# Hybrid encoder trunk: two of the four recurrent units of a layer run their chunks in step, and x is fetched in one layout for its first norm

## The chip, the cores and the metric

The kernel runs on one core of one Trainium2 chip. The metric is the device time of one launch in microseconds (us), as the median of several runs. TensorE (PE in the profile) has a clock of two levels, 1.2 and 2.4 GHz; the profile gives the granted level as a share, 0.50 or 1.00.

## The reference, cut to what matters

Two layers work on x, 256 tokens by 2048 channels in f32. Each layer normalises x, multiplies it by a 2048 by 14784 matrix, and feeds four branches of width 512:

```python
h = _rms_norm(x, norm_g[l])       # x * rsqrt(mean(x*x) + 1e-6) * g
p = h @ w_in[l]
y_a = _rwkv7_bidir(...)           # 8 heads of 64, one scan over tokens in each direction
y_b = _diff_attention(...)        # differential attention
y_c = _mla(...)                   # latent attention
y_d = _mem_attention(...)         # attention into 256 memory tokens
z = sum(sigmoid(merge_b) * ((y_b * silu(gate_b)) @ w_branch[l, b]))
x = x + z @ w_out[l]
```

The recurrent branch y_a updates a 64 by 64 state per head and direction with every token; afterwards each head is normalised over its 64 channels.

## The kernel before, in words

Every large product is done as three fp32r products: `split` writes a rounded high part and the remainder of both operands (for weights the tiles `whi` on ScalarE and `wlo` on VectorE, line 95 in the profile, since a metering wrapper calls the engine there). `main` is the lane of these products. It walks a list of jobs in a fixed order: keys and values of the memory branch (`in_mem_w_kv`, two jobs of 16 contraction tiles), then the products with `w_in`, the small ones of the latent attention, branch products, and `w_out`. A job with `("hT", l)` as its condition is only written into the program once the normalised and transposed x exists.

Beside `main` run seven lanes: norms of the memory, parameters and `z_prep`, norms of x (`x_prep`, for layer 0 `x_first`), tables, attention, latent attention, and the recurrent branch (`rwkv`). They are generators; a loop in `build` takes them in turns, with assumed times for PE, VectorE and ScalarE, and so sets the order in which instructions are written; a scheduler of the framework with priorities sets the final order on each engine. On the chip each engine runs its instructions strictly in that order.

`x_first` in layer 0 needs one factor per token, rsqrt(mean(x*x)+eps). It fetches x twice: as `xT` (channels on partitions, four pieces of 512 KB into tiles U and ygh, which held the memory's pieces until then) and as `x` (tokens on partitions, two pieces of 1 MB into Z). `token_sums` squares and sums the latter on ScalarE in four pieces with an accumulator, takes `rsqrt` of 2 columns on GpSimd with the power operation, and `x_first` then spreads the factor, transposes it on PE (line 161) and copies it to the tile `r4` (`rb`; the profile drops the digit and names it r). All 16 tiles of xT are multiplied by gain and factor on VectorE, and split into T1h and T1l, the moving operands of the first `w_in` job.

`rwkv` calls `rw_unit` for four units of two heads one after another. A unit has a preparation (decay, keys, the products PR, a triangular inverse in `rw_inverse`, whose result is TT), then four steps n over chunks of 64 tokens, in which both directions advance: products R, their copy, products SA with TT, their copies, products SP and Y, and the state update on VectorE. All use PSUM tiles `pr`, of which there are two; Y holds one of them during the steps. Then comes the head norm of the unit.

Start of the launch: small memory fills on GpSimd (`ticks`) pace the first transfers; `tick(i, dst)` lets a transfer start after fill i. The first two memory tiles have raised priority.

Of the kernel before, what the change touches and what calls it, by code (L numbers as in the profile page):

```python
# [10 lines left out]
F32 = mybir.dt.float32  # L11
# [5 lines left out]
ALU = mybir.AluOpType  # L17
# [28 lines left out]
XE = 5.0  # L46
# [66 lines left out]
class Builder:  # L113
# [71 lines left out]
    def setup(self):  # L185
        nc, a = self.nc, self.a
        self.cst = self.cp.tile([128, C_N], F32, name="cst")
        self.ident = self.cst[:, C_ID:C_ID + 128]
        self.G = self.cp.tile([128, 2, 4, 65], F32, name="G")
        self.ticks = [nc.gpsimd.memset(self.G, 1.0).ins]  # L190
        self.ones = self.cp.tile([128, 2], F32, name="ones")
        nc.gpsimd.memset(self.ones, 1.0)
        with self.tc.high_priority(2 * HP):
            nc.scalar.activation(self.small(2), self.ones, AF.Exp)
            warm = self.t("PT", [128, 2, 256], bufs=1)[:, 0]
            nc.vector.memset(warm, 0.0)
# [3 lines left out]
        self.TT = self.cp.tile([128, 2, 4, 64], F32, name="TT")  # L200
        self.ticks.append(nc.gpsimd.memset(self.TT, 0.0).ins)
        self.ST = [self.cp.tile([128, 2, 2, 64], F32, name=f"ST{i}") for i in range(2)]
        for s in self.ST:
# [140 lines left out]
    def mem_prep(self, l):  # L344
# [22 lines left out]
        for i in range(8):  # L367
            if not l and 1 <= i <= 4:
                with self.tc.issue_after(self.last[0]):
                    load(i + 3)  # L370
            if not l and i == 3:
                with self.tc.issue_after(self.fetch):
                    nc.sync.dma_start(self.cst, a["consts"])
            for kk in (2 * i, 2 * i + 1):
                j, k = kk // 4, kk % 4
                with self.tc.high_priority(2 * HP if kk < 4 else 0):
# [24 lines left out]
    def x_first(self):  # L401
# [140 lines left out]
    def main(self):  # L542
# [7 lines left out]
        def prepare(upto):  # L550
            while nxt[0] < len(flat) and nxt[0] <= upto:
# [161 lines left out]
    def e_merge(self, l, b, j):  # L713

        def f(tt, ps):
# [59 lines left out]
    def z_prep(self, l):  # L775

        parts = self.v["zT", l] = []
        for i, tags in enumerate((("q1",), ("k1",), ("V1",), ("iA",), ("X",), ("BK", "qr"), ("T1h",), ("T1l",))):
# [304 lines left out]
    def rwkv(self, l):  # L1083
# [3 lines left out]
        for ft in range(4):  # L1087
            yield from self.rw_unit(l, ft, U)
# [8 lines left out]
    def rw_unit(self, l, ft, U):  # L1097
# [26 lines left out]
        X = self.t("X", [128, 2, 4, 128])  # L1124
        nc.gpsimd.memset(X[64:128, :, 0:4:2], 0.0)
        nc.gpsimd.memset(X[0:64, :, 1:4:2], 0.0)
        pv = self.pr().rearrange("p (a f) -> p a f", a=4)
        for c in range(2):
            self.mm(pv[:, c], v[:, c * 128:c * 128 + 128], cst[:, C_CEN:C_CEN + 128])
        for d in range(2):  # L1130
            self.copy(X[0:64, d, 0:4:2], pv[0:64, 0:2])
            nc.vector.tensor_copy(X[64:128, d, 1:4:2], pv[64:128, 0:2])
# [11 lines left out]
        G = self.G  # L1144
        AR = self.t("S2", [128, 2, 4, 2, 64])
        BKT = self.t("S3", [128, 2, 4, 128])
        PR = [self.t(f"S{d}", [128, 4, 2, 128]) for d in range(2)]
        kds = self.t("kds", [128, 256])
# [10 lines left out]
        for d in range(2):  # L1159
# [55 lines left out]
        yield from self.rw_inverse(PR)  # L1215


        TT = self.TT
        Y = self.pr()[:, :256]
        st = None  # L1220
        for n in range(4):
# [5 lines left out]
            def kp(c):  # L1227
                return slice(64, 128) if c % 2 else slice(0, 64)

            R = self.pr()[:, :128].rearrange("p (h i) -> p h i", h=2)  # L1230
            if n:
                for d, c in dc:
                    self.mm(R[bp(c)].rearrange("p h i -> p (h i)"), AR[:, d, c, 0],
                            st[:, d].rearrange("p h i -> p (h i)"), True, False)
            for hb in range(2):
                hs = slice(hb * 64, hb * 64 + 64)
                for d, c in dc:
                    self.mm(R[bp(c), hb], PR[d][:, ci(c), hb, 0:64], X[:, d, c, hs], not n, n == 0 or hb == 1)
            Rs = self.t("Rs", [128, 2, 64], bufs=2)
            self.copy(Rs, R)  # L1240
            yield
            SA = self.pr()[:, :128].rearrange("p (h i) -> p h i", h=2)
            for hb in range(2):
                for d, c in dc:
                    self.mm(SA[bp(c), hb], TT[bp(c), d, (c // 2) * 2 + hb], Rs[bp(c), hb])
            for d, c in dc:
                o = X[bp(c), d, c].rearrange("p (h i) -> p h i", h=2)
                if d == 0:
                    self.copy(o, SA[bp(c)])
                else:  # L1250
                    nc.vector.tensor_copy(o, SA[bp(c)])
            yield
            if n < 3:
                SP = self.pr()[:, :128].rearrange("p (d i) -> p d i", d=2)
                for d, c in dc:
                    for hb in range(2):
                        hs = slice(hb * 64, hb * 64 + 64)
                        self.mm(SP[hs, d], BKT[:, d, c, hs], X[:, d, c, hs])
            for d, c in dc:
                first, final = (n == 0 and d == 0), (n == 3 and d == 1)  # L1260
                cs = slice(c * 64, c * 64 + 64)
                for hb in range(2):
                    hs = slice(hb * 64, hb * 64 + 64)
                    self.mm(Y[hs, cs], X[:, d, c, hs], PR[d][:, ci(c), hb, 64:128], first, final and not n)
                for hb in range(2):
                    hs = slice(hb * 64, hb * 64 + 64)
                    if n:
                        self.mm(Y[hs, cs], st[:, d, hb], AR[:, d, c, 1], False, final)
            if n < 3:
                o0, o1 = n * 65 + 64, 260 + (3 - n) * 65  # L1270
                gc = G.rearrange("p d c t -> p (d c t)")[:, o0:o1 + 1:o1 - o0]
                new = self.ST[n % 2]
                gb = gc[:, :, None].to_broadcast([128, 2, 64])
                for hb in range(2):
                    hs = slice(hb * 64, hb * 64 + 64)
                    src = SP[hs]
                    if n:
                        nc.vector.tensor_tensor(new[hs, :, hb], src, st[hs, :, hb], op=ALU.add)
                        src = new[hs, :, hb]
                    nc.vector.tensor_tensor(new[hs, :, hb], src, gb[hs], op=ALU.mult)  # L1280
                st = new
            yield


        sq = self.t("sq", [128, 256])
        nc.scalar.activation(sq, Y, AF.Square)
        yg = self.t("r2", [128, 256], bufs=2)
        self.copy(yg, Y, scale=col(P_GG + ft))
        yield
# [11 lines left out]
        bv = self.t("r3", [128, 256], bufs=2)  # L1301
# [5 lines left out]
        nc.vector.tensor_tensor(yg, yg, ps, op=ALU.mult)  # L1307
# [3 lines left out]
    def rw_inverse(self, PR):  # L1311
# [4 lines left out]
        TT = self.TT  # L1316
# [231 lines left out]
```

## Time and profile before

| what | value |
|---|---|
| median of 3 runs | 2039.52 us (2034.0 to 2042.97) |
| profiled execution, its time | 2035.4 us |
| its span (first to last instruction) | 2033.5 us |
| PE busy | 2016.3 us, 99% of the span, 12066 matmuls |
| VectorE, ScalarE, GpSimd busy | 70%, 55%, 8% |
| DMA | 369.45 MB, mean 182 GB/s |

A busy PE in this profile need not be at its peak: the ends of matmuls are modelled, and consecutive ones overlap in the record. What a matmul occupies is read from start to start of its neighbours.

### The profile page before, as it was taken

The page shows a single profiled execution, that of the slowest core. Times are in us where ns is not written, and L with a number is a line of the kernel's source. Part 1 is how long each engine was busy: PE and PEld are TensorE (multiplying, and loading weights), DVE is VectorE, ACT ScalarE, POOL GpSimd, SP SyncE. Part 2 cuts the span into 40 slices and gives each one's busy share as a digit, 9 for nine tenths or more (in the row PEclk, how much of TensorE's full clock was granted, in tenths as well). Part 3 has the DMA queues.
Part 4 walks back from the last instruction along what each step waited for, and adds up shares of the span by engine and source line. Part 5 has one row for each costly group of instructions (what it writes and reads, how often), then busy time and mean ns, then how long its engine had stood idle before and what let it go on. Part 6 is the DMA issues. An engine that isn't in the chain of part 4 may idle for free.

```text
span 2033.5 us, 33805 instructions
## 1 busy us (share of the span) xinstructions
PE 2016.3 (99%) x12066; PEld 1695.8 (83%) x12066; DVE 1417.8 (70%) x3070; ACT 1118.1 (55%) x2317; POOL 152.9 (8%) x174
## 2 busy tenths in 40 slices
PE   8999999999999999999999999999999999999999
PEld 6998997887877888777889988888778778877887
DVE  5878888986587577558565658666656876765664
ACT  5756565655455445446465556765555554444543
POOL 1201100210010000000000010110011001000000
PEclk9999999999999999999999999999999999999999
DMA  8665655566455556656765656455555555665565
GB/s 298 215 183 157 189 173 171 148 186 186 141 181 165 169 171 191 198 171 226 237 191 179 182 156 179 147 164 175 161 181 166 176 157 158 197 200 165 183 201 190
DMA packets 222585, 369.45 MB, mean 182 GB/s; under 512 B 40592, under 2 KB 60816, under 8 KB 221840
## 3 DMA queue, kind: packets, MB, share of 16 engines
q1 hardware_dynamic: 218736, 356.31, 57.8%
q10 hardware_dynamic: 3456, 10.49, 1.3%
q8 instruction: 95, 1.56, 0.3%
q0 software_dynamic: 224, 0.49, 0.2%
q14 instruction: 74, 0.61, 0.1%
HBM read 359.88 MB, written 11.53 MB: 183 GB/s over the span
## 4 chain that ended last, share of the span: by engine, by line
PE 91%; issue 3%; DVE 2%; DMA 2%; ACT 1%; SPq 0%; POOL 0%; ACTq 0%; DVEq 0%; POOLq 0%
PE mm L156 81%; PE pr L156 5%; PE pa L156 3%; PE pa L161 2%; DMA raww<-in_mem_w_kv 1%; DVE wlo L95 1%; PE pr L161 0%; DVE S L95 0%; DMA raww<-in_w_in 0%; DMA U<-in_memT 0%; ACT whi L95 0%; SPq L1375 0%; DVE Z L95 0%; DVE BK L95 0%; POOL small L179 0%
## 5 line engine op out<-in xcount | busy, mean ns | idle before, releaser
L95 ACT ACTIVATE whi<-raww 128x512 fp32r<-128x512 f32 (+2 forms) x1300 | 786.7, 616 | 738.3 <-PE mm L156 407.0
L95 DVE TENSOR_TENSOR wlo<-raww,whi 128x512 fp32r<-128x512 f32 (+2 forms) x1300 | 863.9, 675 | 449.7 <-ACT whi L95 439.2
L156 PE MATMUL mm<-wlo,T1h 128*128 128x512 f32 (+2 forms) x1440 | 564.6, 392 | 2.6 <-DVE wlo L95 2.6
L156 PE MATMUL mm<-whi,T1l 128*128 128x512 f32 (+2 forms) x1472 | 566.1, 388 | 0.0
L156 PE MATMUL mm<-whi,T1h 128*128 128x512 f32 (+2 forms) x1472 | 537.7, 391 | 1.3 <-ACT whi L95 1.2
L156 PEld LDWEIGHTS mm<-whi,T1h 128*128 128x128 f32 x1472 | 275.3, 188 | 57.1 <-ACT whi L95 2.1
L156 PEld LDWEIGHTS mm<-whi,T1l 128*128 128x128 f32 x1472 | 276.5, 188 | 51.8 <-issue 0.3
L156 PEld LDWEIGHTS mm<-wlo,T1h 128*128 128x128 f32 x1440 | 270.6, 188 | 57.8 <-DVE wlo L95 5.1
L156 PE MATMUL mm<-T1l,whi 128*128 128x256 f32 x960 | 272.4, 285 | 0.4 <-DVE T1l L95 0.4
L156 PE MATMUL mm<-T1h,wlo 128*128 128x256 f32 x960 | 272.6, 286 | 0.0
L156 PE MATMUL mm<-T1h,whi 128*128 128x256 f32 x960 | 272.5, 285 | 0.0
L156 PEld LDWEIGHTS mm<-T1l,whi 128*128 128x128 f32 x960 | 183.6, 191 | 1.6 <-DVE T1l L95 0.6
L156 PEld LDWEIGHTS mm<-T1h,whi 128*128 128x128 f32 x960 | 183.6, 192 | 1.2
L156 PEld LDWEIGHTS mm<-T1h,wlo 128*128 128x128 f32 x960 | 183.0, 191 | 0.8
L156 PE MATMUL mm<-wlo,ygh 128*128 128x512 f32 (+1 forms) x296 | 116.5, 396 | 0.0
L156 PE MATMUL mm<-whi,ygl 128*128 128x512 f32 (+1 forms) x296 | 115.6, 393 | 0.0
L156 PE MATMUL mm<-whi,ygh 128*128 128x512 f32 (+1 forms) x296 | 110.0, 395 | 0.0
L156 PE MATMUL mm<-whi,S 128*128 128x512 f32 x256 | 86.5, 414 | 5.0 <-ACT whi L95 4.8
L179 POOL TENSOR_TENSOR small<-small,cst 128x4 f32<-128x4 f32 (+3 forms) x46 | 52.3, 1139 | 514.1 <-DVE small L95 430.1
L156 PEld LDWEIGHTS mm<-whi,ygl 128*128 128x128 f32 x296 | 55.6, 188 | 12.3 <-issue 1.0
L156 PEld LDWEIGHTS mm<-whi,S 128*128 128x128 f32 x256 | 50.0, 198 | 19.1 <-ACT whi L95 7.6
L156 PEld LDWEIGHTS mm<-whi,ygh 128*128 128x128 f32 x296 | 55.6, 188 | 12.3 <-issue 1.0
(279 smaller groups left out, 2165.8 us busy)
## 6 DMA issues: line engine op xcount, KB each, us to landing
raww<-in_w_in SPq DMA_DIRECT2D x432, 512.0 KB, 3.6
raww<-in_w_branch SPq DMA_DIRECT2D x64, 512.0 KB, 4.5
raww<-in_w_out SPq DMA_DIRECT2D x64, 512.0 KB, 4.6
raww<-in_mem_w_kv SPq DMA_DIRECT2D x29, 512.0 KB, 3.6
raww<-in_w_in SPq DMA_DIRECT2D x16, 384.0 KB, 3.6
raww<-in_w_in SPq DMA_DIRECT2D x16, 320.0 KB, 3.7
raww<-in_w_in SPq DMA_DIRECT2D x16, 256.0 KB, 2.8
Z<-in_x ACTq DMA_DIRECT2D x2, 1024.0 KB, 6.9
```

The lines of the kernel that those rows point to most:

```text
L95: return g(out, *args, **kw)
L156: return self.nc.tensor.matmul(out, lhsT=lhsT, rhs=rhs, start=start, stop=stop).ins
L161: self.nc.tensor.transpose(out, in_, self.ident[:k, :k])
L179: self.nc.gpsimd.tensor_tensor(ss, ss, self.cst[:, C_MH:C_MH + n], op=ALU.pow)
```

## The change

- `x_first` fetches only xT. It squares the four pieces on ScalarE (128 by 1024 each), adds them on VectorE down to 128 by 256, sums over partitions with one product with a matrix of ones, scales, and applies the power of -0.5 on GpSimd to the whole 128 by 256 tile, against a tile filled with -0.5.
- The third and fourth unit of each layer are prepared one after the other; then `rw_chunks` takes both through their steps: in each step the products R of both units, then SA of both, then SP and Y of both, with PSUM tiles that hold both. The second of the pair has its own G, TT and ST, and uses S4, S5, S6 of the latent attention (and kds2, BKT, iA), so it waits for `("gatefree", l, 1)`, the end of the latent attention's heads.
- BKT, the transposed keys, is made for three chunks of a direction, not four, since the last is not used.
- The group norm's gain moves from the copy of Y into the later multiplication. The recurrent branch's merge gates go to q1, k1, V1, and `z_prep` takes its tiles in another order.
- At the start, ticks of the paced transfers are one fill earlier, and only two, no longer four, of the first memory tiles have raised priority. The scratch of GpSimd's transfers is halved.

```diff
-        self.G = self.cp.tile([128, 2, 4, 65], F32, name="G")
-        self.ticks = [nc.gpsimd.memset(self.G, 1.0).ins]
+        self.G = [self.cp.tile([128, 2, 4, 65], F32, name=f"G{i}") for i in range(2)]
+        self.ticks = [nc.gpsimd.memset(self.G[0], 1.0).ins]
...
+        with self.tc.issue_after(self.ticks[-1]):
+            nc.gpsimd.memset(self.G[1], 1.0)
+            for s in (self.TT[1], *self.ST[1]):
+                nc.gpsimd.memset(s, 0.0)
...
-                self.tick((0, 1, 4, 7)[i], dst[:, 0, 0:1])
+                self.tick((0, 0, 3, 6)[i], dst[:, 0, 0:1])
...
-        rs = self.small(2)
-        yield from self.token_sums(a["x"][0], rs)
-        ex = self.t("sq", [128, 2, 128])
-        nc.vector.tensor_copy(ex, rs[:, :, None].to_broadcast([128, 2, 128]))
+        sq = self.t("T1l", [128, 4, 1024])
+        one = self.t("Rs", [128, 128], bufs=2)
+        nc.gpsimd.memset(one, 1.0)
+        yield XE
+        for j in range(4):
+            with self.tc.issue_after(self.last[0]):
+                nc.scalar.activation(sq[:, j], X[j].rearrange("p k t -> p (k t)"), AF.Square)
+            if j % 2:
+                with self.tc.issue_after(self.last[1]):
+                    nc.vector.tensor_tensor(sq[:, j - 1], sq[:, j - 1], sq[:, j], op=ALU.add)
+            yield
+        nc.vector.tensor_tensor(sq[:, 0], sq[:, 0], sq[:, 2], op=ALU.add)
+        nc.vector.tensor_tensor(sq[:, 0, 0:512], sq[:, 0, 0:512], sq[:, 0, 512:1024], op=ALU.add)
+        nc.vector.tensor_tensor(sq[:, 0, 0:256], sq[:, 0, 0:256], sq[:, 0, 256:512], op=ALU.add)
         ps = self.pa()[:, :256]
-        for tt in range(2):
-            self.tr(ps[:, tt * 128:tt * 128 + 128], ex[:, tt])
+        self.mm(ps, one, sq[:, 0, 0:256])
         rb = self.t("r4", [128, 256], bufs=1)
-        self.copy(rb, ps)
+        nc.vector.tensor_scalar(rb, ps, 1.0 / D, EPS, op0=ALU.mult, op1=ALU.add)
+        half = self.t("sq", [128, 256])
+        nc.gpsimd.memset(half, -0.5)
+        nc.gpsimd.tensor_tensor(rb, rb, half, op=ALU.pow)
         yield
...
-                                self.tick((0, 0, 3, 4, 5, 6)[2 * i + q], raw[:, q, 0:1])
+                                self.tick((0, 0, 2, 3, 4, 5)[2 * i + q], raw[:, q, 0:1])
...
-                    self.v["sgs", j] = self.t(("S4", "S5", "S6")[j], [128, 2, 512])
+                    self.v["sgs", j] = self.t(("q1", "k1", "V1")[j], [128, 2, 512])
...
-        for ft in range(4):
-            yield from self.rw_unit(l, ft, U)
+        for fts in ((0,), (1,), (2, 3)):
+            units = []
+            for i, ft in enumerate(fts):
+                if i:
+                    yield from self.until(("gatefree", l, 1))
+                units.append((yield from self.rw_prep(l, ft, U, i)))
+            yield from self.rw_chunks(units)
+            for i, ft in enumerate(fts):
+                yield from self.rw_finish(l, ft, U, units[i])
...
-            for c in range(4):
-                self.tr(ps[:, c], BK[:, c // 2, 2 * (c % 2):2 * (c % 2) + 2].rearrange("p s t -> p (s t)"))
-            self.copy(BKT[:, d], ps)
+            for n in range(3):
+                c = 3 - n if d else n
+                self.tr(ps[:, n], BK[:, c // 2, 2 * (c % 2):2 * (c % 2) + 2].rearrange("p s t -> p (s t)"))
+            self.copy(BKT[:, d], ps[:, 0:3])
...
+    def rw_chunks(self, units):
...
+        for n in range(4):
...
+            R = self.pr()[:, :m * 128].rearrange("p (u h i) -> p u h i", u=m, h=2)
+            for u, (X, AR, BKT, PR, kds, G, TT, ST, _) in enumerate(units):
...
+            Rs = self.t("r1", [128, m, 2, 64], bufs=2)
+            self.copy(Rs, R)
+            yield
+            SA = self.pr()[:, :m * 128].rearrange("p (u h i) -> p u h i", u=m, h=2)
+            for u, (X, AR, BKT, PR, kds, G, TT, ST, _) in enumerate(units):
+                for hb in range(2):
+                    for d, c in dc:
+                        self.mm(SA[bp(c), u, hb], TT[bp(c), d, (c // 2) * 2 + hb], Rs[bp(c), u, hb])
...
-        nc.vector.tensor_tensor(yg, yg, ps, op=ALU.mult)
+        nc.vector.scalar_tensor_tensor(yg, yg, col(P_GG + ft), ps, op0=ALU.mult, op1=ALU.mult)
```

## Rows read from the trace of the kernel before

**Rows 1.** The page, part 1: busy time, share of the span, instructions.

```profile
PE 2016.3 (99%) x12066; PEld 1695.8 (83%) x12066; DVE 1417.8 (70%) x3070; ACT 1118.1 (55%) x2317; POOL 152.9 (8%) x174
```

**Rows 2.** Timeline of PE, start of the launch: start, duration, instructions, idle before.

```profile
5.62 1.22 PE L156 MATMUL mm<-whi,S 128*128 128x512 f32 x2 [0.65 <-ACT whi L95]
...
13.07 0.63 PE L156 MATMUL mm<-whi,S 128*128 128x512 f32 x1
...
14.54 0.39 PE L156 MATMUL mm<-wlo,S 128*128 128x512 f32 x1
...
34.25 1.21 PE L156 MATMUL mm<-whi,S 128*128 128x512 f32 x4 [1.88 <-ACT whi L95]
...
42.87 0.74 PE L156 MATMUL mm<-whi,S 128*128 128x512 f32 x2 [1.62 <-ACT whi L95]
...
56.42 0.38 PE L161 MATMUL pa<-cst,sq 128*128 128x128 f32 x2
...
61.76 0.40 PE L156 MATMUL mm<-T1h,whi 128*128 128x256 f32 x2
```

**Rows 3.** Windows: length, PE, PEld, DVE, ACT, POOL busy, clock, DMA share, GB/s.

```profile
42.00:56.00 14.00, 13.13 (x49) 10.25 (x50) 10.23 (x26) 10.14 (x18) 0.75 (x1) 0.88 0.69 222
```

**Rows 4.** Timeline of ACT and its DMA queue, where x is fetched and squared.

```profile
25.39 0.33 ACTq L388 DMA_DIRECT2D Z<-in_x  x1
...
33.98 0.33 ACTq L409 DMA_DIRECT2D ygh<-in_xT  x1
...
47.52 1.04 ACT L95 ACTIVATE Z<-Z 128x1024 f32<-128x1024 f32 x1
```

**Rows 5.** Timeline of DVE, the memory's last pieces and the normalisation of x.

```profile
29.83 0.88 DVE L95 SCALAR_TENSOR_TENSOR S<-ygh,gains,S 128x256 fp32r<-128x256 f32 x2
...
57.55 1.67 DVE L95 SCALAR_TENSOR_TENSOR U<-U,gains,r 128x256 f32<-128x256 f32 x4
...
61.36 1.29 DVE L95 TENSOR_TENSOR T1l<-U,T1h 128x512 fp32r<-128x512 f32 x2
```

**Rows 6.** Timeline of POOL: the power operation (L179, L1295) at four widths, an addition (L1195).

```profile
1266.80 0.56 POOL L179 TENSOR_TENSOR small<-small,cst 128x1 f32<-128x1 f32 x1 [16.08 <-DVE small L95]
...
582.42 0.71 POOL L179 TENSOR_TENSOR small<-small,cst 128x2 f32<-128x2 f32 x1 [5.08 <-DVE small L95]
...
358.72 1.01 POOL L1295 TENSOR_TENSOR small<-small,cst 128x4 f32<-128x4 f32 x1 [5.47 <-DVE small L95]
...
472.40 1.64 POOL L179 TENSOR_TENSOR small<-small,cst 128x8 f32<-128x8 f32 x1 [20.57 <-DVE small L95]
...
186.81 0.78 POOL L1195 TENSOR_TENSOR kds<-kds,r 128x256 f32<-128x256 f32 x1 [10.67 <-DVE r L95]
```

**Rows 7.** Timeline of PE, chunk steps of the third unit in layer 0.

```profile
683.62 0.28 PE L156 MATMUL mm<-T1h,wlo 128*128 128x256 f32 x1
683.83 0.45 PE L156 MATMUL pr<-Rs,TT 64*64 64x64 f32 x8
684.21 0.39 PE L156 MATMUL mm<-T1h,whi 128*128 128x256 f32 x1
...
686.83 0.28 PE L156 MATMUL mm<-T1h,whi 128*128 128x256 f32 x1
687.04 0.34 PE L156 MATMUL pr<-S,X 128*64 128x64 f32 x4
...
687.93 0.38 PE L156 MATMUL mm<-T1l,whi 128*128 128x256 f32 x1
```

**Rows 8.** Timeline of PE, transposes into BKT and what follows.

```profile
749.37 0.60 PE L161 MATMUL pr<-cst,BK 128*128 128x128 f32 x4
749.81 0.60 PE L156 MATMUL pr<-LW,wup 128*128 128x256 f32 x2
```

**Rows 9.** Timelines of PE and DVE at the end of layer 0's recurrent lane.

```profile
907.62 0.39 PE L156 MATMUL mm<-whi,ygh 128*128 128x512 f32 x1
...
911.19 0.42 DVE L95 TENSOR_TENSOR ygl<-U,ygh 128x256 fp32r<-128x256 f32 x1
```

More of the change, by code (lines that the diff above doesn't have):

```diff
@@ L199, in setup @@
                 self.nc.tensor.matmul(ps, lhsT=warm[:, :128], rhs=warm, start=True, stop=True)
[L200 to L203, printed above, removed]
+        self.TT = [self.cp.tile([128, 2, 4, 64], F32, name=f"TT{i}") for i in range(2)]
+        self.ticks.append(nc.gpsimd.memset(self.TT[0], 0.0).ins)
+        self.ST = [[self.cp.tile([128, 2, 2, 64], F32, name=f"ST{u}{i}") for i in range(2)] for u in range(2)]
+        for s in self.ST[0]:
             at = nc.gpsimd.memset(s, 0.0).ins
@@ L375, in mem_prep @@
                 j, k = kk // 4, kk % 4
-                with self.tc.high_priority(2 * HP if kk < 4 else 0):
+                with self.tc.high_priority(2 * HP if kk < (4 if l else 2) else 0):
                     self.split(T[j][:, k], T[4 + j][:, k], X[j][:, k], scale=g[:, kk:kk + 1])
@@ L777, in z_prep @@
         parts = self.v["zT", l] = []
-        for i, tags in enumerate((("q1",), ("k1",), ("V1",), ("iA",), ("X",), ("BK", "qr"), ("T1h",), ("T1l",))):
+        for i, tags in enumerate((("X",), ("iA",), ("BK", "qr"), ("q1",), ("T1h",), ("k1",), ("T1l",), ("V1",))):
             yield from self.until(("z", l, i // 2))
@@ L1095, in rwkv, with rw_values, rw_prep @@
         self.ev.add(("Ufree", l))
-    def rw_unit(self, l, ft, U):
+    def rw_values(self, v, tag):
+        nc, cst = self.nc, self.cst
+        X = self.t(tag, [128, 2, 4, 128])
+        nc.gpsimd.memset(X[64:128, :, 0:4:2], 0.0)
+        nc.gpsimd.memset(X[0:64, :, 1:4:2], 0.0)
+        pv = self.pr().rearrange("p (a f) -> p a f", a=4)
+        for c in range(2):
+            self.mm(pv[:, c], v[:, c * 128:c * 128 + 128], cst[:, C_CEN:C_CEN + 128])
+        for d in range(2):
+            self.copy(X[0:64, d, 0:4:2], pv[0:64, 0:2])
+            nc.vector.tensor_copy(X[64:128, d, 1:4:2], pv[64:128, 0:2])
+        return X
+    def rw_prep(self, l, ft, U, pos):
         nc, a = self.nc, self.a
@@ L1123, in rw_unit @@
         nc.gpsimd.tensor_tensor(inv, inv, cst[:, C_MH:C_MH + 4], op=ALU.pow)
[L1124 to L1132, printed above, removed]
+        if not pos:
+            X = self.rw_values(v, "X")
         yield
@@ L1142, in rw_unit @@
         yield
[L1144 to L1148, printed above, removed]
+        G, TT = self.G[pos], self.TT[pos]
+        AR = self.t(("S2", "S6")[pos], [128, 2, 4, 2, 64])
+        BKT = self.t(("S3", "BKT")[pos], [128, 2, 3, 128])
+        PR = [self.t(f"S{4 * pos + d}", [128, 4, 2, 128]) for d in range(2)]
+        kds = self.t(("kds", "kds2")[pos], [128, 256])
         def ci(c):
@@ L1207, in rw_unit @@
             ps = self.pr().rearrange("p (m t) -> p m t", m=4)
-            for c in range(4):
-                self.tr(ps[:, c], BK[:, c // 2, 2 * (c % 2):2 * (c % 2) + 2].rearrange("p s t -> p (s t)"))
-            self.copy(BKT[:, d], ps)
+            for n in range(3):
+                c = 3 - n if d else n
+                self.tr(ps[:, n], BK[:, c // 2, 2 * (c % 2):2 * (c % 2) + 2].rearrange("p s t -> p (s t)"))
+            self.copy(BKT[:, d], ps[:, 0:3])
             yield
         nc.vector.scalar_tensor_tensor(kds, kds, col(P_RK + ft), r, op0=ALU.mult, op1=ALU.mult)
[L1215 to L1220, printed above, removed]
+        yield from self.rw_inverse(PR, TT)
+        if pos:
+            X = self.rw_values(v, "iA")
+            yield
+        return X, AR, BKT, PR, kds, G, TT, self.ST[pos]
+    def rw_chunks(self, units):
+        nc = self.nc
+        m = len(units)
+        bank = self.pr()
+        Y = [bank[:, u * 256:u * 256 + 256] for u in range(m)]
+        for u, w in enumerate(units):
+            w += (Y[u],)
+            units[u] = w
+        st = [None] * m
         for n in range(4):
@@ L1225, in bp @@
                 return slice(0, 64) if c % 2 else slice(64, 128)
[L1227 to L1238, printed above, removed]
@@ L1239, in rw_unit, with ci @@
-            Rs = self.t("Rs", [128, 2, 64], bufs=2)
+            def ci(c):
+                return c % 2 * 2 + c // 2
+            R = self.pr()[:, :m * 128].rearrange("p (u h i) -> p u h i", u=m, h=2)
+            for u, (X, AR, BKT, PR, kds, G, TT, ST, _) in enumerate(units):
+                if n:
+                    for d, c in dc:
+                        self.mm(R[bp(c), u].rearrange("p h i -> p (h i)"), AR[:, d, c, 0],
+                                st[u][:, d].rearrange("p h i -> p (h i)"), True, False)
+                for hb in range(2):
+                    hs = slice(hb * 64, hb * 64 + 64)
+                    for d, c in dc:
+                        self.mm(R[bp(c), u, hb], PR[d][:, ci(c), hb, 0:64], X[:, d, c, hs], not n, n == 0 or hb == 1)
@@ L1240, in rw_unit @@
+            Rs = self.t("r1", [128, m, 2, 64], bufs=2)
             self.copy(Rs, R)
             yield
-            SA = self.pr()[:, :128].rearrange("p (h i) -> p h i", h=2)
-            for hb in range(2):
-                for d, c in dc:
[L1245 to L1251, printed above, removed]
+            SA = self.pr()[:, :m * 128].rearrange("p (u h i) -> p u h i", u=m, h=2)
@@ new lines, in rw_chunks @@
+            for u, (X, AR, BKT, PR, kds, G, TT, ST, _) in enumerate(units):
+                for hb in range(2):
+                    for d, c in dc:
+                        self.mm(SA[bp(c), u, hb], TT[bp(c), d, (c // 2) * 2 + hb], Rs[bp(c), u, hb])
+            for u, w in enumerate(units):
+                for d, c in dc:
+                    o = w[0][bp(c), d, c].rearrange("p (h i) -> p h i", h=2)
+                    if d == 0:
+                        self.copy(o, SA[bp(c), u])
+                    else:
+                        nc.vector.tensor_copy(o, SA[bp(c), u])
@@ L1252, in rw_unit @@
             yield
             if n < 3:
-                SP = self.pr()[:, :128].rearrange("p (d i) -> p d i", d=2)
+                SP = self.pr()[:, :m * 128].rearrange("p (u d i) -> p u d i", u=m, d=2)
+                for u, (X, AR, BKT, PR, kds, G, TT, ST, _) in enumerate(units):
+                    for d, c in dc:
+                        for hb in range(2):
+                            hs = slice(hb * 64, hb * 64 + 64)
+                            self.mm(SP[hs, u, d], BKT[:, d, n, hs], X[:, d, c, hs])
@@ L1255, in rw_unit @@
+            for u, (X, AR, BKT, PR, kds, G, TT, ST, Yu) in enumerate(units):
                 for d, c in dc:
+                    first, final = (n == 0 and d == 0 and u == 0), (n == 3 and d == 1 and u == m - 1)
+                    cs = slice(c * 64, c * 64 + 64)
                     for hb in range(2):
                         hs = slice(hb * 64, hb * 64 + 64)
[L1258 to L1268, printed above, removed]
+                        self.mm(Yu[hs, cs], X[:, d, c, hs], PR[d][:, ci(c), hb, 64:128], first, final and not n)
+                    for hb in range(2):
+                        hs = slice(hb * 64, hb * 64 + 64)
+                        if n:
+                            self.mm(Yu[hs, cs], st[u][:, d, hb], AR[:, d, c, 1], False, final)
@@ L1269, in rw_unit @@
             if n < 3:
                 o0, o1 = n * 65 + 64, 260 + (3 - n) * 65
[L1271 to L1280, printed above, removed]
@@ L1281, in rw_unit @@
-                st = new
-            yield
[L1285 to L1288, printed above, removed]
-        yield
+                for u, (X, AR, BKT, PR, kds, G, TT, ST, _) in enumerate(units):
+                    gc = G.rearrange("p d c t -> p (d c t)")[:, o0:o1 + 1:o1 - o0]
+                    new = ST[n % 2]
+                    gb = gc[:, :, None].to_broadcast([128, 2, 64])
+                    for hb in range(2):
+                        hs = slice(hb * 64, hb * 64 + 64)
+                        src = SP[hs, u]
+                        if n:
+                            nc.vector.tensor_tensor(new[hs, :, hb], src, st[u][hs, :, hb], op=ALU.add)
+                            src = new[hs, :, hb]
+                        nc.vector.tensor_tensor(new[hs, :, hb], src, gb[hs], op=ALU.mult)
+                    st[u] = new
@@ new lines, in rw_chunks, with rw_finish, col @@
+            yield
+        for u, w in enumerate(units):
+            sq = self.t("r3", [128, 256], bufs=2)
+            nc.scalar.activation(sq, Y[u], AF.Square)
+            yg = self.t("r2", [128, 256], bufs=2)
+            self.copy(yg, Y[u])
+            units[u] = w[:-1] + (sq, yg)
+        yield
+    def rw_finish(self, l, ft, U, unit):
+        nc, cst = self.nc, self.cst
+        cols = self.v["cols", l]
+        v = U[:, 8 + ft]
+        kds, sq, yg = unit[4], *unit[-2:]
+        b2 = cst[:, C_B2:C_B2 + 2]
+        def col(p):
+            return cols[:, p:p + 1]
```

7 lines of the change are left out of this document (3 added, 4 removed).

## Prediction

> **What bounds the kernel now.** I read the page first: PE is busy 2016.3 of 2033.5 us [rows 1], so only 17 us are idle by the record, and an edit counts only if it takes work off PE, closes a gap of PE or opens one. VectorE (70%) and ScalarE (55%) have slack on average, GpSimd is at 8%. Then PE's timeline at the start: two long gaps, 1.88 us before 34.25 and 1.62 us before 42.87, both while ScalarE waited for weights of the memory job [rows 2]; after the second the clock is at its lower level for a while: 0.88 on average over 14 us, so 14 x 0.12 / 0.5 = 3.4 us at half rate, 1.7 us lost [rows 3]. At the very start matmuls run at half rate until about 13.8 (records of 0.63 us at 13.07, 0.39 at 14.54 [rows 2]). From 61.76 PE works on normalised x (T1h). That is the place to watch: nothing that `main` issues after the memory job can run without T1h and T1l, and PE takes its instructions in order.
>
> The other views: ScalarE and its queue for when x is fetched and squared [rows 4], VectorE for what follows the factor [rows 5], GpSimd for the power operation [rows 6], and PE's neighbours start to start for batches of small matmuls [rows 7, 8].
>
> **The power on 256 columns.** Before, GpSimd takes the power of 2 columns here. Undisturbed instances of the same operation last 0.56, 0.71, 1.01 and 1.64 us for 1, 2, 4 and 8 columns [rows 6]. From 4 to 8 columns that is 0.63/4 = 0.157 us a column, from 2 to 4 it is 0.15, from 1 to 2 it is 0.15: a straight line, 0.38 us plus 0.157 us a column. At 256 columns: 0.38 + 256 x 0.157 = 40.6 us. The trace has no power that wide. The lower bound is an addition on the same engine at exactly this shape, 0.78 us [rows 6]. I take the line, because it is the same operation, has four points on it, and shows no flattening.
>
> The Trainium skill's rule speaks for the lower end: the page "GPSIMD Engine Reference", section 3.1, gives about 2.6 cycles an element for a two-input operation, and section 1 a clock of 1.2 GHz, which makes 256 x 2.6 / 1.2 = 0.55 us, an estimate from that page. By it this edit would cost PE nothing, and the kernel would come out faster (rival B). The addition agrees with it; the power at 8 columns, 1.64 us where the rule leaves 0.02 us beside the fixed cost, does not.
>
> **When the power starts.** Before, the squares of Z are interleaved with weight pieces on ScalarE and end at 47.52 + 1.04 = 48.6 [rows 4]. The two 1 MB pieces of x disappear (issued from 25.39 on, among the pieces of xT [rows 4]), so the weights that PE waited for come sooner: up to 1.88 + 1.62 + 1.7 = 5.2 us of progress by then. Squares of xT at the same places end near 43.5. The last quarter of xT can be there: its buffer is free when VectorE has split the memory's last piece, 29.83 + 0.88 = 30.7 [rows 5], while before its issue waited until 33.98 [rows 4]. On VectorE two 512-wide subtractions take 1.29 us [rows 5], so additions of 1024, 1024, 512 and 256 columns take about 1.2 + 1.2 + 0.65 + 0.35 = 3.4 us, and two weight pieces in between 1.3 us: 48.2. Then one product and one scaling, 0.8 us, if PE comes to it at once; before, PE came to the corresponding transposes at 56.42 [rows 2], 51.2 without the gaps. I take 51.5 as the power's start; bounds 42 (squares right behind the last piece) and 56.
>
> So `rb` is there at 51.5 + 40.6 = 92.1. Then a pair of multiplications (1.67/4 = 0.42 us each), the high part and the remainder (0.65 us each [rows 5]): first products at 94.3, where they began at 61.76 [rows 2]. PE would be 32.5 us late; with the 4.5 us that lay between the end of normalisation's factor and 61.76 in the old order it would be 35. I take 33; bounds from the start of the power and the shorter and longer tail: 23 and 39. PE has finished the memory job by about 57 and has nothing else. Behind the waiting multiplications on VectorE stand the weight remainders and the tables, behind the power on GpSimd the rotary products and the memory's factor; all of them serve work that comes after x is normalised, so they shift with PE and add nothing.
>
> After that idle time PE restarts at the lower clock: 1.7 us lost after the 1.62 us gap [rows 3], some 4 us lost at the start of the launch (half rate from its first products at 5.62 to about 13.8 [rows 2]). I take 2.5, bounds 1.7 and 4. The gaps of rows 2 close but give nothing: PE only waits longer for x.
>
> **Units in step.** The same products are issued, but a layer has 4 steps x 3 batches = 12 batches fewer, 24 in all. A batch of 8 costs 684.21 - 683.62 = 0.59 us between its neighbours, less 0.12 for the neighbour's own product: 0.47. The batch at 686.83 to 687.93, 24 matmuls with the rows left out, costs 1.10 - 0.12 = 0.98 [rows 7]. So 16 more cost 0.51, 0.032 each, and 0.47 - 8 x 0.032 = 0.21 is the price of having a batch at all: entry and draining. 24 x 0.21 = 5.0 us gained; bounds 24 x 0.09 (the entry alone: 683.83 - 683.62 - 0.12) = 2.2 and, if the second batch fitted wholly beside the first, 24 x 0.38 = 9 us.
>
> **BKT for three chunks.** 8 units x 2 directions = 16 transposes fewer at (749.81 - 749.37)/4 = 0.11 us [rows 8]: 1.8 us gained. The copy gets shorter on ScalarE, which has slack.
>
> **Edits at nothing.** The two old transposes of the factor against one product of 256 columns: 0.2 us each way. The new fills on GpSimd come behind the paced ones, on an engine 8% busy. Ticks one fill earlier start the first transfers about half a microsecond sooner, and the raised priority of two memory tiles moves only the order of the first pieces; whatever PE wins before 57 us it waits for x. The gain in the multiplication replaces one VectorE operation by one of the same size. q1, k1, V1 for the merge gates and the new order of `z_prep`: their former users, the heads of the differential attention, are done before branch 1's products, hence before these gates; cover gone, each would cost a wait of one product. S4 to S6 for the fourth unit: the latent attention must have ended, and that unit is the last of four. The halved scratch concerns a handful of small transfers.
>
> **Sum.** +33 + 2.5 - 5.0 - 1.8 = +28.7 us on the profiled execution's own time of 2035.4: 2064. That execution lies 4.1 us under the median of the runs; on the median the same sum gives 2039.5 + 28.7 = 2068. Bounds together: 23 + 1.7 - 9 - 1.8 = +14 and 39 + 4 - 2.2 - 1.8 = +39, that is 2054 to 2078 from the median.
>
> **Rivals.**
> A (forecast, 0.80): x is late by the power operation; 2068.
> B (0.12): the power is cheap, like the addition. Then `rb` is there near 52.5, x is ready when PE has finished the memory job, PE starts on it some 5 us earlier, and with 5.0 and 1.8 the kernel takes 2039.5 - 11.8 = 2028. For it: the addition's 0.78 us. Against: the line over four widths. A and B part where the delay eats the 6.8 us of the recurrent edits: 51.5 + p + 2.2 = 61.76 + 6.8 gives p = 15 us, 0.06 us a column; the trace has 0.157.
> C (0.04): the recurrent lane becomes late. In layer 0 its last remainder is written at 911.19 while PE already works on its first products from 907.62 on [rows 9]; there is no slack to lose. If the pair, or its wait for the latent attention, ended the lane 10 us later in both layers, 20 us would be added; with a cheap power 2048. Against: one loop over steps replaces two, so the lane should end earlier.
> D: the batches do not merge because the scheduler puts large products between the two units. The 5 us fall away: 2073 with A, inside its range and counted there.
> The remaining 0.04 are mixtures.
>
> **Chances.** A measurement of this kernel can tell about 0.5% (10 us) from no change. A is slower throughout. B lies at -0.58%, near the bound: 0.07 faster, 0.05 the same. C and the rest: 0.01 faster, 0.05 the same, 0.02 slower. Faster 0.08, same 0.10, slower 0.82. The likeliest case's own range is 2054 to 2078; to hold 8 in 10 I take 2042 to 2079.
>
> **What would show it.** In the profile after: one power of 128x256 on GpSimd, started near 51.5, of about 40 us; an idle stretch of PE of about 37 us, from about 57 to about 94, and half clock behind it; no large gap between 32 and 43; groups of 16 matmuls `pr<-Rs,TT` in the second half of each layer, 0.7 us each; 48 transposes into BKT instead of 64. The prediction is wrong if the power takes under 15 us, or if something between the squares and the power holds it until far beyond 56 us, or if PE has idle time near the end of a layer.

## The result, and the profile after

The kernel after takes 2084.74 us (median, 2084.51 to 2085.59) against 2038.22 us before on the same chip: a ratio of 1.0228 [1.0205, 1.0252], 46.5 us slower. The prediction had the sign and the main cause, and its 2068 (2042 to 2079) was too low. The profiled execution after took 2085.59 us, its span is 2083.8.

The page of the kernel after, engines and two lines of slices, against [rows 1]:

```profile
PE 2019.1 (97%) x12050; PEld 1688.0 (81%) x12050; DVE 1426.2 (68%) x3072; ACT 1116.5 (54%) x2304; POOL 191.9 (9%) x180
PE   8199999999999999999999999999999999999999
PEclk9599999999999999999999999999999999999999
```

The span is 50 us longer and PE's busy time only 2.8: the difference is almost all idle time of PE, and it lies in the second slice (52 to 104 us). The granted clock of that slice is 0.5, the lower level. The waits of PE name it (us in total, times, longest):

```profile
PE mm L156 <- ACT T1h L95: 43.4, 1, 43.4
PE mm L156 <- DVE T1l L95: 4.7, 1, 4.7
PE mm L156 <- ACT whi L95: 4.2, 5, 2.4
PE pr L161 <- DVE S L95: 2.8, 1, 2.8
```

So follow that one wait from end to end. The timeline of ACT after, which answers to [rows 4], has the last piece's fetch and square, and the first high part:

```profile
28.93 0.33 ACTq L413 DMA_DIRECT2D ygh<-in_xT  x1
...
43.00 1.04 ACT L95 ACTIVATE T1l<-ygh 128x1024 f32<-128x1024 f32 x1
...
99.88 0.63 ACT L95 ACTIVATE T1h<-U 128x512 fp32r<-128x512 f32 x1 [41.83 <-DVE U L95]
```

The timeline of DVE: the last addition, the scaling behind the product with ones, then the normalisation ([rows 5] before):

```profile
51.08 0.42 DVE L95 TENSOR_TENSOR T1l<-T1l 128x256 f32<-128x256 f32 x1
...
57.16 0.42 DVE L95 TENSOR_SCALAR r<-pa 128x256 f32<-128x256 f32 x1 [0.23 <-PE pa L156]
...
98.97 4.84 DVE L95 SCALAR_TENSOR_TENSOR U<-U,gains,r 128x256 f32<-128x256 f32 x12 [40.03 <-POOL r L435]
103.72 1.67 DVE L95 SCALAR_TENSOR_TENSOR ygh<-ygh,gains,r 128x256 f32<-128x256 f32 x4
105.31 3.69 DVE L95 TENSOR_TENSOR T1l<-U,T1h 128x512 fp32r<-128x512 f32 x6
```

The timeline of POOL, the power:

```profile
57.67 41.27 POOL L435 TENSOR_TENSOR r<-r,sq 128x256 f32<-128x256 f32 x1 [24.43 <-DVE r L95]
```

And the timeline of PE, around the product with ones, the two waits for x, a stretch of large products, and a step of the two units together ([rows 2, 7] before):

```profile
56.30 0.39 PE L156 MATMUL mm<-whi,S 128*128 128x512 f32 x1
56.53 0.59 PE L156 MATMUL pa<-T1l,Rs 128*128 128x256 f32 x2
...
100.56 0.80 PE L156 MATMUL mm<-T1h,whi 128*128 128x256 f32 x2 [43.44 <-ACT T1h L95]
...
106.05 0.58 PE L156 MATMUL mm<-T1l,whi 128*128 128x256 f32 x1 [4.68 <-DVE T1l L95]
...
110.48 0.38 PE L156 MATMUL mm<-T1l,whi 128*128 128x256 f32 x1
110.69 0.28 PE L156 MATMUL mm<-T1h,wlo 128*128 128x256 f32 x1
...
683.79 0.39 PE L156 MATMUL mm<-whi,T1l 128*128 128x512 f32 x1
684.02 0.63 PE L156 MATMUL mm<-whi,T1h 128*128 128x512 f32 x2
...
684.49 0.40 PE L156 MATMUL mm<-wlo,T1h 128*128 128x512 f32 x1
...
685.19 0.39 PE L156 MATMUL mm<-whi,T1l 128*128 128x512 f32 x1
...
856.37 0.40 PE L156 MATMUL mm<-wlo,ygh 128*128 128x512 f32 x1
856.69 0.68 PE L156 MATMUL pr<-r,TT 64*64 64x64 f32 x16
857.31 0.50 PE L156 MATMUL mm<-whi,ygl 128*128 128x512 f32 x1
```

Read it as a relay. The sum is ready on VectorE at 51.50, but PE multiplies it by ones only at 56.53, behind the last product of the memory job. The power runs from 57.67 to 98.94. Then VectorE does all 16 multiplications (98.97 to 105.39) before its first remainder, so that PE gets T1h at 100.56, does what needs no T1l, and waits again until 106.05. Its next products run at half rate until about 110.5. PE begins steady work on x at 106.05, where it was 61.76 [rows 2].

One more thing is in these rows, away from the start. From 683.79 to 685.19 lie six steps of 512 columns (from the start of one product to the start of the next): 0.233 us each. In the kernel before, three of them take 0.68, 0.227 each:

```profile
672.14 0.39 PE L156 MATMUL mm<-whi,T1h 128*128 128x512 f32 x1
...
672.82 0.39 PE L156 MATMUL mm<-whi,T1h 128*128 128x512 f32 x1
```

There are 5,808 products of this width in either kernel, though not all of them change by as much.

### The profile page after: what moved, and what is told of

It is laid out like the page before. It is cut to its first block, busy times and chain, and to the rows that moved or that the text cites. A ratio compares the mean times of both kernels' runs of the same rounds, so it can differ in the third digit from the quotient of the medians.

```text
span 2083.8 us, 33769 instructions
## 1 busy us (share of the span) xinstructions
PE 2019.1 (97%) x12050; PEld 1688.0 (81%) x12050; DVE 1426.2 (68%) x3072; ACT 1116.5 (54%) x2304; POOL 191.9 (9%) x180
## 4 chain that ended last, share of the span: by engine, by line
PE 63%; DMA 1%; DVE 0%; issue 0%; ACT 0%; DVEq 0%; SPq 0%; ACTq 0%
PE mm L156 57%; PE pr L156 3%; PE pa L156 1%; PE pa L161 1%; DMA kkn<-in_diff_lambda 0%; PE pr L161 0%; DMA raww<-in_w_branch 0%; DMA TT<-yd 0%; DMA raww<-in_w_in 0%; ACT whi L95 0%; DVEq L1605 0%; DVE wlo L95 0%; DVE S L95 0%; DVE sq L95 0%; SPq L579 0%
## 5 line engine op out<-in xcount | busy, mean ns | idle before, releaser
L179 POOL TENSOR_TENSOR small<-small,cst 128x4 f32<-128x4 f32 (+3 forms) x45 | 55.4, 1232 | 413.9 <-DVE small L95 390.5
L156 PEld LDWEIGHTS mm<-wlo,ygh 128*128 128x128 f32 x296 | 55.6, 188 | 11.0 <-issue 0.3
```

The costliest lines, as they stand in the source:

```text
L156: return self.nc.tensor.matmul(out, lhsT=lhsT, rhs=rhs, start=start, stop=stop).ins
L179: self.nc.gpsimd.tensor_tensor(ss, ss, self.cst[:, C_MH:C_MH + n], op=ALU.pow)
```

## The experiments

One kernel takes up to 3 us more or less on another chip. So each gain or loss below is taken against runs of the kernel before on the same chip: 2036.02 us beside `e1_narrow`, `e3_units` and the two `pad32` kernels, 2035.99 beside `e5_narrow_z`, `a_squares_z` and `a_order`, 2039.19 beside `a_align`, `b_misalign`, `best` and `e3_single`. The kernel after lost 46.5 us in this way.

**The wide power and the recurrent part, each without the other.** `e1_narrow` keeps everything of the change but takes the power on 2 columns, in the layout with tokens on partitions. `e3_units` has the recurrent part alone; it fetches x and paces the first transfers as before. The edit of `e1_narrow`:

```diff
-        self.mm(ps, one, sq[:, 0, 0:256])
...
-        nc.gpsimd.tensor_tensor(rb, rb, half, op=ALU.pow)
+        for tt in range(2):
+            self.mm(ps[:, 2 * tt:2 * tt + 2], sq[:, 0, tt * 128:tt * 128 + 128], self.ones)
+        rs = self.small(2)
+        nc.vector.tensor_scalar(rs, ps[:, 0:4:2], 1.0 / D, EPS, op0=ALU.mult, op1=ALU.add)
+        nc.gpsimd.tensor_tensor(rs, rs, self.cst[:, C_MH:C_MH + 2], op=ALU.pow)
```

> x still fetched in one layout and squared and added as in the changed kernel, but the sum over partitions goes to two columns with tokens on partitions, the power is taken of 2 columns, and the factor is spread and transposed as before. Theory 1 (the 41.3 us power makes x late): PE's 43 us wait goes away, first products with x near 62 us, time about 2084.7 - 44 = 2041. Rival 1 (squares, additions and their place in the queues make x late, whatever the power's width): x stays more than 15 us late, 2055 or more.

> Only the recurrent part of the change (pairs of units, three chunks of BKT, buffers); x fetched and normalised as before, transfers paced as before. Theory 1: the recurrent part gains 5.0 + 1.8 us as forecast, 2031. Rival 2 (after the late x the changed kernel loses 6 us more by the end, and the paired units cost them): 2044. If instead the pace of large products depends on where tiles lie in SBUF, the sum of small matmuls (pr) falls by 6 us and the step of 512-column products tells the rest.

Measured: `e1_narrow` 2043.52 us, 1.0038 [1.0024, 1.0051] of before; `e3_units` 2022.8 us, 0.9937 [0.992, 0.9953]. With the narrow power a loss of 7.5 us is left of 46.5, 39 us less, and the recurrent part is a gain of 13.2 us, about twice the expected one. So most of the loss is the width of one operation. The timelines of POOL and PE in `e1_narrow`:

```profile
59.09 0.72 POOL L432 TENSOR_TENSOR small<-small,cst 128x2 f32<-128x2 f32 x1 [45.06 <-DVE small L95]
```
```profile
62.95 0.79 PE L156 MATMUL mm<-T1h,whi 128*128 128x256 f32 x2 [2.30 <-ACT T1h L95]
...
68.43 0.58 PE L156 MATMUL mm<-T1l,whi 128*128 128x256 f32 x1 [4.69 <-DVE T1l L95]
```

But with x late by 68.43 - 61.76 = 6.7 us and a gain of 13.2, this kernel should have been 6.5 us faster than before, and it was 7.5 slower. 14 us were still without a cause, and the longer step of the large products was the suspect.

**Is it where a tile lies?** The change alters the order and size of tiles in SBUF. Two kernels shift all work tiles, weights and x alike, by 32 bytes, before and after:

```diff
+        pad = self.cp.tile([128, 8], F32, name="pad")
+        nc.gpsimd.memset(pad, 0.0)
```

> The kernel before with a tile of 32 bytes a partition put among the constants, so that the weight tiles and T1h, T1l lie 32 bytes further; nothing else. Theory 3 (the step of large products depends on where operands start): steps of 512-column products with T1h leave 227 ns and those of 256-column products leave 120 ns, time changes by 5 us or more either way. Rival 3 (the steps 234 and 117 of the changed kernel have another cause): 227 and 120 stay, 2038.

> The changed kernel with the same 32 bytes added. Theory 3: steps of 512-column products leave 234 ns, 256-column ones leave 117 ns, and the time moves by 5 us or more. Rival 3: 234 and 117 stay, 2084.7.

Measured: `b_pad32` 2036.99 us, 1.0002 [0.9991, 1.0013], `a_pad32` 2084.0 us, 1.0237 [1.0222, 1.0253]: no change beyond noise in either. The absolute place is not the cause. Two others put the squares into Z (`sq = self.t("Z", [128, 4, 1024])`), so that T1h and T1l lie side by side as before:

> The kernel with the power of 2 columns, and the squares written to tile Z and not to T1l, so that T1h and T1l are laid out one behind the other as in the kernel before. Theory 4: steps go back from 234 and 117 to 227 and 120 ns, the time falls by 12 to 17 us from 2043.5 to 2027 to 2031. Rival 4: the steps stay, 2043.

> The changed kernel with its power of 256 columns; only the squares go to Z and not to T1l. Theory 4: steps of 227 and 120 ns, 2084.7 - 16 = 2069. Rival 4: 2084.7.

Measured: `e5_narrow_z` 2042.76 us, 1.0031 [1.0022, 1.0041], `a_squares_z` 2083.22 us, 1.0228 [1.0211, 1.0245]. The step stayed at 234 ns, so the order of these tiles is not the cause either.

**Power and operand places by themselves.** `m_parts` leaves the trunk out. It takes the power at ten widths, and runs the same pattern of fp32r products with the weight tiles always at the same places, multiples of 64 bytes, and the two operands that stand for T1h and T1l at five pairs of places. As in the kernel, these two are the stationary operand in products of 512 columns and the moving one in products of 256. In bytes from the start of the tile the pairs are: the first pair (44544, 60928), both multiples of 64, then (45536, 20960), (44512, 20960), (44512, 60896) and (20960, 45536), all 32 above a multiple of 64.

> Parts alone: the whole computation of the trunk is left out. GpSimd takes the power of 1 to 512 columns in doubling widths and one addition of 256; PE runs the kernel's pattern of large products (96 each) with the two moving or stationary operands at several distances from the weights in SBUF, first those of the kernel before, then those of the changed kernel. Theory 1: power lasts 0.38 + 0.157 us a column at every width, 40.6 us at 256 and 80.8 at 512. Theory 4 (the step of large products depends on where T1h and T1l lie) in its simplest form: 227 and 120 ns for the first layout, 234 and 117 ns for the second. Rival 4: the same steps for all layouts, so the cause needs the rest of the kernel.

The groups of POOL by shape, then timelines of PE: at 512 columns a stretch of the first pair at the full clock, one of the second, and the row of the last two pairs; at 256 columns the rows of the first two pairs:

```profile
L1561 POOL TENSOR_TENSOR res<-base,half 128x512 f32<-128x512 f32 x1 | 82.2, 82157 | 0.1
L1561 POOL TENSOR_TENSOR res<-base,half 128x256 f32<-128x256 f32 x1 | 41.2, 41242 | 0.1
...
L1561 POOL TENSOR_TENSOR res<-base,half 128x64 f32<-128x64 f32 x1 | 10.5, 10547 | 0.1
...
L1561 POOL TENSOR_TENSOR res<-base,half 128x8 f32<-128x8 f32 x1 | 1.6, 1635 | 0.1
...
L1562 POOL TENSOR_TENSOR res<-base,half 128x256 f32<-128x256 f32 x1 | 0.7, 742 | 0.1
```
```profile
29.76 6.51 PE L1580 MATMUL b<-R 128*128 128x512 f32 x28
...
49.71 6.46 PE L1580 MATMUL b<-R 128*128 128x512 f32 x27
...
86.61 45.47 PE L1580 MATMUL b<-R 128*128 128x512 f32 x192 [0.15 <-DVE o L1584]
132.23 11.78 PE L1577 MATMUL b<-R 128*128 128x256 f32 x96 [0.15 <-DVE o L1584]
144.50 11.62 PE L1577 MATMUL b<-R 128*128 128x256 f32 x96 [0.49 <-DVE o L1584]
```

The power is a straight line up to 512 columns: (82.16 - 41.24)/256 = 0.160 us a column. A record of one such product is 0.39 us long, so the first pair's stretch of 28 products has steps of (6.51 - 0.39)/27 = 0.227 us at the full clock, and the second pair's 27 products have (6.46 - 0.39)/26 = 0.233. The last three pairs step like the second (median 234 ns, mean 233). At 256 columns it is the other way round: 120 ns for the first pair, and for the rest a median of 117 and a mean of 118. These are the two sets of steps of the kernels before and after. The first and the fourth pair differ by 32 bytes only, and hardly anything else runs but a power on GpSimd: it is the start of one operand against the other.

**The same in the kernel.** In `a_align`, a tile of 32 bytes ahead of T1l brings T1h and T1l to the same remainder by 64 bytes as the weights. `b_misalign` puts the same tile into the kernel before, ahead of T1h, and so takes them apart.

```diff
+        nc.gpsimd.memset(self.t("padw", [128, 8]), 0.0)
         sq = self.t("T1l", [128, 4, 1024])
```

> The changed kernel with its power of 256 columns and a tile of 32 bytes a partition placed between the weight tiles and T1l, T1h, so that weights and x operands start at the same remainder modulo 64 bytes, as in the kernel before. Theory 5 (the step of large products depends on whether their two operands have the same remainder modulo 64): 227 and 120 ns a step, 2084.7 - 16 = 2069. Rival 5: 234 and 117, 2084.

> The kernel before with the same 32 bytes placed between the weight tiles and T1h, T1l, so that the remainders differ. Theory 5: 234 and 117 ns a step, 2036 + 16 = 2052. Rival 5: 227 and 120, 2036.

Measured: `a_align` 2070.0 us, 1.0144 [1.0127, 1.0162], 30.8 us more than before and so 15.7 us less than the kernel after lost. `b_misalign` 2048.67 us, 1.0038 [1.0025, 1.0051], 9.5 us more than before. The tile T1h in `a_align` (engine, operation, count: duration in ns min/median/max, first and last start), and the same stretch of PE's timeline as above:

```profile
L156 PE MATMUL mm<-whi,T1h x1472: 302/389/585, 190.3 to 2053.8; 128*128 128x512 f32 x168, 128*128 128x384 f32 x8, 128*128 128x320 f32 x8
```
```profile
684.37 0.39 PE L156 MATMUL mm<-whi,T1l 128*128 128x512 f32 x1
684.59 0.39 PE L156 MATMUL mm<-wlo,T1h 128*128 128x512 f32 x1
684.82 0.39 PE L156 MATMUL mm<-whi,T1l 128*128 128x512 f32 x1
685.05 0.62 PE L156 MATMUL mm<-whi,T1h 128*128 128x512 f32 x2
685.50 0.39 PE L156 MATMUL mm<-wlo,T1h 128*128 128x512 f32 x1
```

From 684.37 to 685.50 lie five steps, 0.226 each. Summed from start to start over the whole trace, the products of 512 columns take 1392.0 us in the kernel after and 1369.9 in `a_align`, those of 256 columns 363.6 and 368.4: 17.3 us less in all, and the two profiled spans are 17.0 apart. The same tile in the kernel after and in `b_misalign`:

```profile
L156 PE MATMUL mm<-whi,T1h x1472: 304/394/588, 190.0 to 2070.6; 128*128 128x512 f32 x168, 128*128 128x384 f32 x8, 128*128 128x320 f32 x8
```
```profile
L156 PE MATMUL mm<-whi,T1h x1472: 305/395/628, 142.2 to 2036.5; 128*128 128x512 f32 x168, 128*128 128x384 f32 x8, 128*128 128x320 f32 x8
```

A median of 389 or of 394 to 395 ns in this view sorts the kernels. By the addresses in the programs all 13 follow one rule: 389 where weights and T1h, T1l have the same remainder by 64 bytes (before, `e3_units`, `b_pad32`, `a_align`, and `best` and `e3_single` below), 394 where it differs by 32 (after and the others). The remainders of weights and of T1h, T1l are 32 and 32 before, 0 and 32 after, 0 and 0 in `a_align`, 32 and 0 in `b_misalign`: it is not enough that one of them is a multiple of 64. `b_misalign` paid less than the 16 us expected: its 512-column products got slower by 19.1 us (1385.0 to 1404.1 in all) and its 256-column products faster by 6.6 (357.2 to 350.6).

**The order at the start.** `a_order` raises the priority of the last additions, the product with ones, the scaling and the power, and orders the multiplications of each piece behind the remainder of the piece before:

```diff
+        with self.tc.high_priority(2 * HP):
...
-                with self.tc.issue_after(self.last[1]):
+                with self.tc.issue_after(done):
...
-            self.split(hi[:, 2 * j:2 * j + 2], lo[:, 2 * j:2 * j + 2], xs)
+            done = self.split(hi[:, 2 * j:2 * j + 2], lo[:, 2 * j:2 * j + 2], xs)[1]
```

> The changed kernel with its power of 256 columns, but the last additions, the product over partitions and the scaling have raised priority, and each multiplication of a piece of x is ordered behind the remainder of the piece before. Theory 1 with its two mis-sized places (the power starts 6 us late because its product stands behind the whole memory job on PE; PE waits again for the remainder, which stands behind all 16 multiplications on VectorE): the power starts near 52 instead of 57.7, the second wait of 4.7 us is under 1.5 us, together 8 to 10 us less, 2075. Rival 1b (the power's length alone counts): 2084.

Measured: 2080.5 us, 1.0215 [1.0199, 1.023], 44.5 us more than before where the kernel after lost 46.5: 2 us less, of the size of the noise, and not the 8 to 10 expected. PE's steady work on x begins 1.7 us earlier, at 104.36. The timeline of PE, with the only wait for x that is left, and that of POOL:

```profile
60.33 0.59 PE L156 MATMUL pa<-T1l,Rs 128*128 128x256 f32 x2
...
104.36 0.80 PE L156 MATMUL mm<-T1h,whi 128*128 128x256 f32 x2 [43.44 <-ACT T1h L95]
```
```profile
61.46 41.27 POOL L436 TENSOR_TENSOR r<-r,sq 128x256 f32<-128x256 f32 x1 [25.54 <-DVE r L95]
```

The wait for the remainder is gone, as expected. The other half missed: the product with ones stayed behind the memory job in PE's order, which itself ended later, and the power began 3.8 us later than in the kernel after. An earlier product wasn't reached by any kernel here with the wide power.

**What of the recurrent part gains.** `e3_single` is `e3_units` with the units one after another: all the new buffers and three BKT chunks, but no pairs.

```diff
-        for fts in ((0,), (1,), (2, 3)):
+        for fts in ((0,), (1,), (2,), (3,)):
```

> The recurrent part with its buffers, three chunks of BKT and gate tiles, but the third and fourth unit go one after the other like the first two. Theory 1: only the saving of batches and of waits that the pairing gives is lost, 5 us or more of the 13.2: 2028 to 2032. Rival 6 (the gain comes from the other buffers and the new order of z_prep, not from the pairing): 2023.

Measured: 2040.09 us, 1.0 [0.999, 1.0009], 0.9 us more than before and above the 2028 to 2032 expected. The whole gain is gone, so it is the pairs: -13.2 us with them against +0.9 without, 14 us. BKT's 16 transposes show no gain; the 1.8 us predicted for them would lie at the edge of the interval.

**Everything together.** `best` is `e1_narrow` with the 32 bytes and with the order of `a_order`'s remainders:

> x in one layout with the power of 2 columns, each remainder of x ordered before the next piece's multiplication, the 32 bytes of the first run of this call, and the paired units. Theories 1 and 5 together: 2043.5 - 16 (step) - 5 (second wait for the remainder) - 2 (clock) = 2020, a little under the paired units alone (2022.8). Rival: fetching x once still makes x late; above 2025.

Measured: 2024.22 us, 0.9919 [0.9904, 0.9934], 15.0 us less than before. The expected 2020 was reckoned from times of `e1_narrow`'s chip and stood for 16.0 less. It beats both kernels, but against the 13.2 us of `e3_units` the 1.8 more are within the two intervals: that fetching x in one layout gains anything, even with a narrow power, is not shown.

## Why the prediction was too low

**The width of the power: right.** A line over 1, 2, 4 and 8 columns [rows 6] gave 40.6 us, and it took 41.27. The rule of the Trainium skill ("GPSIMD Engine Reference", section 3.1) that made rival B, 0.55 us, does not hold for the power. The addition of the same shape took 0.74 us in `m_parts`, near the rule's 0.55. Rival B falls.

**Its start: 6 us too early.** The sum's arithmetic was right: ready at 51.50 on VectorE. What failed is the step "one product and one scaling, 0.8 us, if PE comes to it at once": I let PE come to it where it had come to the old transposes, less the gaps. It came behind the whole memory job, and the power began at 57.67, beyond the bound of 56.

**Behind it: 5 us too short.** The prediction let the first pair's high part and remainder follow its multiplication, 2.2 us. VectorE had all 16 multiplications ordered first: 106.05 - 98.94 = 7.1. Together with the start, PE was 44.3 us late where the sum had 33. I had priced the operations of one piece, and not the order in which the others stand on the engine.

**The clock: right.** PE at half rate from 106.05 to about 110.5 costs some 2.2 us, predicted 2.5. Windows of the profile after (columns as in [rows 3]), with the clock in the third column from the right:

```profile
57.00:101.00 44.00, 0.56 (x3) 0.44 (x2) 3.31 (x8) 2.01 (x5) 41.27 (x1) 0.53 0.16 61
101.00:112.00 11.00, 6.32 (x35) 6.02 (x35) 10.29 (x22) 5.35 (x9) 0.00 (x0) 0.56 0.02 3
```

**The recurrent part: right sign, half the size.** -13.2 measured, -6.8 predicted. The batches merged as said (16 products at 856.69, 0.68 us), so D falls. From 130 us on the trace of before has 184 batches between large products that hold products into `pr` alone, worth 107.6 us beyond the steps of the large ones, and that of `e3_units` has 158, worth 103.9: 3.7 us where 5.0 was predicted. Some 6.9 us more came from stalls between two large products of 512 columns (31.1 us over their normal step before, 24.2 in `e3_units`, 36.2 in `e3_single`). The prediction had priced the batches and not what pairs leave to other engines; which engine these stalls waited on isn't settled.

**The terms that were absent.** No step of the prediction asked where the new tiles put T1h and T1l. It cost 15.7 us, by `a_align`. With it the sum is 44.3 + 2.2 + 15.7 - 13.2 = 49.0, and 46.5 was measured; the 2.5 us between are within the ratio's interval, which spans 42 to 51 us. Without it a loss of 30.8 us stands where 28.7 was forecast, but that closeness is luck in part, two errors of opposite sign: 11 us too little for x, 6 too little gain.

**The edits at nothing.** The gates, `z_prep`, and the wait for the latent attention show no new wait in PE's list beyond one of 2.8 us, for S at 749 us, which `e3_units` has too (2.7). Rival C falls. That one wait costs more than it seems. In the kernel after it comes from VectorE, which stood still for 5.26 us for a small transfer (`diff_lambda`) and so emptied a tile `pr` into S late. Behind it PE's clock is at half rate for 3.4 us, which makes 4.5 us lost in all. In the kernel before, VectorE waited 1.35 us for this transfer, and no wait for VectorE's S stands in PE's list. VectorE's row, then the window behind the wait:

```profile
747.46 0.29 DVE L95 TENSOR_TENSOR kkn<-kkn 128x128 f32<-128x128 f32 x1 [5.26 <-DMA kkn<-in_diff_lambda]
```
```profile
749.00:752.40 3.40, 3.39 (x16) 3.39 (x17) 2.26 (x4) 1.45 (x3) 0.00 (x0) 0.50 0.18 43
```

`e3_units` has the same wait of VectorE (5.24 us), so its gain of 13.2 us is what is left after such a loss.

## What to carry to other kernels

Price an operation by its kind and its width: a factor for each token is taken in the layout in which it has few columns, and spread afterwards. Then ask at which place in PE's order the product stands that such a chain needs, and what is ordered between the late value and its first user. After any change of tiles, compare the step of the untouched large products in both profiles first, and where it has moved, bring the two operands of fp32r products back to the same remainder by 64 bytes. Last, compare times only with runs of the old kernel on the same chip.

## What the runs showed of the hardware that was not expected

- An fp32r product of 512 columns takes 227 ns from start to start when its two operands begin at the same remainder by 64 bytes, and a median of 234 when they are 32 bytes apart; at 256 columns it is 120 and 117. `m_parts` shows it with constant operands, and `a_align` and `b_misalign` in the kernel. Why the sign turns is open: with the width the operands change places too, the weights being the moving operand at 512 columns and the stationary one at 256. Remainders other than 0 and 32 were not tried.
- GpSimd's power costs 0.160 us a column of 128 partitions with no flattening up to 512 columns (82.2 us), 56 times an addition at 256 columns.
- Interleaving two independent chains of small products gave 14 us for four chains in two pairs (`e3_units` against `e3_single`), where the batches that it spared explain about a quarter.
